# A hybrid decoder layer on one core: the sixteen buffers of the normalized x spaced 4160 bytes apart instead of 4096, with one buffer less in two other rings

## The chip, the core and the metric

The kernel runs on one core of a Trainium2 chip. The metric is device time in microseconds (us) of one execution, as a median over runs. On-chip memory has 128 partitions; every buffer below is counted in bytes of one partition.

## The reference, cut to what matters

One decoder layer over a sequence of 2048 tokens of width 1024, all in float32:

```python
u = rmsnorm(h, norm_mix_w);  proj = u @ w_in
# four heads of a gated linear recurrence (hq, hf, hi, hg), chunk by chunk
o_hg = rmsnorm(hgrn2_chunkwise(q, k, v, log_f)) * silu(hg)
# eight heads of sliding-window attention (window 128) with a sink logit
o_att = sliding_window_attention_with_sinks(aq, ak, av, sinks)
h = h + concat(o_hg, o_att) @ w_out
v = rmsnorm(h, norm_ffn_w)
gate = causal_depthwise_conv(v @ w_gate, conv_w, conv_b)
h = h + (silu(gate) * (v @ w_up)) @ w_down
return rmsnorm(h, final_norm_w)
```

## The kernel before, in words

The sequence is done in two halves of 1024 tokens (`HALF`), channels on the partitions. Each half is a mixing stage (the four recurrence heads of `hgrn`, interleaved with the four attention steps of `attend`), the output projection `out_proj`, the gate and up projections `gate_up`, and the down projection `down`, which also loads the x of the next half.

**Precision by splitting.** A float32 operand is kept as two tiles, a rounded high part and the remainder (`split`, `prep`, `split_into`). Each product is three matmuls: high by high (L790, L1000), remainder of the moving operand (L791, L1001), remainder of the weights (L792, L1002). In `unit` (L190 to L209) all three stand in L208, with the two 512-column halves of x behind each other. In the profile's `out<-in` the moving operand stands first and the weights second: `hq<-XH,whi` streams XH through the array with weights whi.

**The x buffers.** `new_x` (L211) takes one buffer from the ring `xh` and one from the ring `xl` of the pool `xp`, eight each (`KT`), 4096 bytes a buffer. They hold XH and XL, the scaled x of the mixing stage. The same sixteen buffers are taken again later under other names: by `Operands.get` (L636) for the operands T2, T3, B22 and T4 of the feed-forward (in the profile T and B), and by `prep_piece` in `down` (L953) for the reloaded activations (xhd, xld). B11, T1 and B21 live elsewhere, in the rings `xh2` and `xl2` of the feed-forward's pool. `project_v` (L601) is the one place where XH and XL are the weights and a prepared weight streams past them.

**Where buffers lie.** Pools follow one another in memory: const, x, w, h, small, then the pool of the stage (`mix0`, `ffn0`, `mix1`, `ffn1`). x, w and h hold nothing but buffers of 4096 bytes: inv, xh and xl, then raw, hi and lo, then the eight slots `m`. So in the program before, every one of these starts at the same place modulo 4096: the first xh buffer at byte 28992, which is 320 modulo 4096, and the xl buffers, raw, whi, wlo and the slots at 320 as well. The small pool shifts what comes behind it: xh2 and xl2 start at 1088 modulo 4096. The ring `ga` of the feed-forward has two buffers of `2 + HALF` floats (4104 bytes, laid out at a distance of 4128): they begin at bytes 220224 and 224352. The first is a multiple of 64, the second lies 32 behind a multiple of 64. `ga` serves as a gate tile and, in `down`, as a home of weights for every third piece (L958, `k % 3 == 2`; `gad` in the profile: high part in the first buffer, remainder in the second).

**The level keys.** Within a recurrence head, `hgrn` goes through seven levels m = 1, 2, 4 ... 64 (L503). For m < 32 and the first three heads of a half, `pairs` (L475) copies every second run of K into a tile KK of 2048 bytes on ScalarE (L479) and runs four matmuls on it (L482, two passes each in the trace). Then Q is updated (L522, VectorE, after those matmuls), K (L523, after the copy) and the gates F (L529); `place_pairs` copies half of the result (`moved`, L489), sends it through a DMA issued from ScalarE (L492, and L494 for m = 1), and writes both halves into ST (L498, L501). KK has `KB` = 2 buffers, so the copy of one level can be made while the matmuls of the level before still have theirs to read. That makes 5 copies a head, 30 in all, and 24 times that one level hands over to the next.

**The small ring.** `ut` has `UT` = 7 buffers of 2048 bytes: the copies out of PSUM in `pair_unit` (s1, u2, s5, u3, L797), the squares of the statistics (sq, fsq, L238), t1 (L695), v7 (L677), and S1, S2 and S4 of the first weight pair (L744).

The order of instructions on each engine's queue is made by the tile framework when the program is built: it simulates the program with its own costs and gives out buffers as they come free (`schedule_with_timeline_sim=True`), so the number of buffers of a ring takes part in the order.

Of the kernel before, what the change touches and what calls it, by code (L numbers as in the profile page):

```python
# [9 lines left out]
F32R = mybir.dt.float32r  # L10
# [7 lines left out]
P = 128  # L18
D = 1024
KT = D // P  # L20
S = 2048
HALF = 1024
# [15 lines left out]
BEHIND = {1: {0: 1}, 2: {0: "pu", 2: "po", 5: "pot"}}  # L38
LEVELS = [1, 2, 4, 8, 16, 32, 64]
NEG = -1.0e30  # L40
UT = 7
RAW = 3
VB = 2
KB = 2
WARM = 12
LV = 4

# [2 lines left out]
def hymba_layer(ctx: ExitStack, tc: tile.TileContext, a: dict, out: bass.AP):  # L50
    nc = tc.nc

    def pool(name, bufs=1, space=None, stack=ctx, **kw):
        if space is not None:
            kw["space"] = space
        return stack.enter_context(tc.tile_pool(name=name, bufs=bufs, **kw))

    cp = pool("const")
    xp = pool("x")
# [14 lines left out]
    def halves():  # L74
        return [(b, slice(b * 512, (b + 1) * 512)) for b in range(NB)]
# [133 lines left out]
        return o  # L209

    def new_x():  # L211
        return (xp.tile([P, HALF], F32R, tag="xh", name="XH", bufs=KT),
                xp.tile([P, HALF], F32R, tag="xl", name="XL", bufs=KT))

    def split(src, w=None, eng=None, dst=None):

        h, l = dst or new_x()
        if w is None:
            nc.scalar.copy(h, src)
            (eng or nc.vector).tensor_tensor(l, src, h.bitcast(F32), op=ALU.subtract)  # L220
        else:
            nc.scalar.activation(h, src, AF.Identity, scale=w)
            nc.vector.scalar_tensor_tensor(l, src, w, h.bitcast(F32), op0=ALU.mult, op1=ALU.subtract)
        return h, l
# [43 lines left out]
    def inv_tile():  # L268
        return xp.tile([P, HALF], F32, tag="inv", name="invb", bufs=1)
# [5 lines left out]
    def load(hf, X, stage, W=None):  # L275

        st = Stats(inv_tile())
        xt = []

        def part(kt, c):  # L280
            nc.sync.dma_start(xt[kt][:, c], a["xT"][kt, :, hf * HALF + c.start:hf * HALF + c.stop])
            split(xt[kt][:, c], nmw[:, kt:kt + 1], dst=[t[:, c] for t in X[kt]])

        for kt in range(KT):
            xt.append(stage())
            X.append(new_x())
            if W is not None and kt == 0:

                parts = [lambda c=c: part(0, c) for _, c in halves()]
                W.append(prep(a["w_att"][ATT_J], parts=(slice(0, P), slice(P, D)), between=parts))  # L290
                for p_ in parts:
                    p_()
            else:
                part(kt, slice(0, HALF))
            if W is not None and kt == 1:
                W.append(prep(a["w_att"][ATT_J + 1]))

            if W is None:
                st.add(xt[kt])
            elif kt >= 3:  # L300
                st.add(xt[kt - 3])
            yield st
        for kt in range(KT - 3, KT) if W is not None else ():
            st.add(xt[kt])
# [38 lines left out]
    def attend(hf, j, X, invb, KS, V, mix, p):  # L343
# [58 lines left out]
        for g, sc in enumerate(scs):  # L402
            pm = []
            for kv in range(2):
                pm.append([p.tile([P, 4, P], F32, tag="pp", name=n, bufs=4) for n in ("po", "pp")])
                pt = ps("at", "ppt")
                for i in range(4):
                    nc.tensor.transpose(pt[:, i * P:(i + 1) * P], sc[:, kv, i], ident)
                ptv = pt.rearrange("p (i q) -> p i q", i=4)
                for dst, mk in zip(pm[kv], (C.ownT, C.prevT)):  # L410
                    nc.vector.tensor_tensor(dst, ptv, mk.unsqueeze(1).to_broadcast([P, 4, P]), op=ALU.mult)
            oT = ps("at", "poT")
            for i in range(4):
                n = g * 4 + i
                noprev = hf == 0 and n == 0
                for prev in range(1 if noprev else 2):
                    for kv in range(2):
                        r = rows(kv)
                        nc.tensor.matmul(oT[r, i * P:(i + 1) * P], V[:, n + 1 - prev, r], pm[kv][prev][:, i],
                                         start=prev == 0, stop=noprev or prev == 1)  # L420
            gs = slice(g * 512, (g + 1) * 512)
            if j < ATT_J - 1:
                nc.scalar.copy(qT[:, gs], oT)
                mix[4 + j] = qT
            else:
                if g == 0:
                    mix[4 + j] = new_x()
                h, l = mix[4 + j]
                nc.scalar.copy(h[:, gs], oT)
                nc.vector.tensor_tensor(l[:, gs], oT, h[:, gs].bitcast(F32), op=ALU.subtract)  # L430
            yield

    def hgrn(hf, h, X, invb, vs, WG, mix, p, fu=None):
# [41 lines left out]
        def pairs():  # L475


            KK = p.tile([P, HALF // 2], F32, tag="KK", name="KK", bufs=KB)
            nc.scalar.copy(KK.rearrange("p (r b c m) -> p r c b m", r=TT // 2, c=2, m=m),  # L479
# [138 lines left out]
    def split_into(h, l, src, eng=None):  # L618
        return (nc.scalar.copy(h, src),  # L619
                (eng or nc.vector).tensor_tensor(l, src, h.bitcast(F32), op=ALU.subtract))  # L620
# [25 lines left out]
    def out_proj(hf, M, p):  # L646
# [4 lines left out]
        st = Stats(acc)  # L651
        sts = [Stats(acc[:, bs], lambda: p.tile([P, 512], F32, tag="ut", name="sq", bufs=UT)) for _, bs in halves()]
        ops = Operands(p)
# [5 lines left out]
        for d in range(KT):  # L659
# [5 lines left out]
            if d == KT - 2:  # L665
# [3 lines left out]
                                  lambda n: p.tile([P, D], F32R, tag="ga", name=n, bufs=2),  # L669
                                  lambda n: p.tile([P, 512], F32, tag="ut", name=n, bufs=UT))  # L670
            if d >= len(W):
# [4 lines left out]
            u = v[d - 4] if d >= 4 else None  # L676
            w = [t[:, bs] if d < KT - 1 else p.tile([P, 512], F32, tag="ut", name="v7", bufs=UT) for _, bs in halves()]  # L677
            sums = []
# [14 lines left out]
            if d < 4:  # L693
                split_into(*ops.get("B11", d), t[:, lo])
                t1 = p.tile([P, 512], F32, tag="ut", name="t1", bufs=UT)  # L695
                nc.vector.tensor_tensor(t1, t[:, hi], t[:, lo], op=ALU.subtract)
# [77 lines left out]
    def pair_unit(W, ops, p, evac, then={}, behind_first=None):  # L774
# [20 lines left out]
        def out(o, name):  # L795
            t = p.tile([P, 512], F32, tag="ut", name=name, bufs=UT)
            copied[:] = [nc.scalar.copy(t, o)]  # L797
            return t
# [119 lines left out]
    def down(hf, kept, acts, p):  # L918
# [89 lines left out]
        for k, (name, _, _, j) in enumerate(todo):  # L1008
            if k + 2 < len(todo):
                ready[k + 2] = prep_piece(k + 2)  # L1010
            if j == 0:
# [6 lines left out]
                if name == "P3":  # L1018
                    acc = inv_tile() if final else wp.tile([P, HALF], F32, tag="raw", name="sums", bufs=RAW)
                    s1, s2 = [Stats(acc[:, bs], lambda: p.tile([P, 512], F32, tag="ut", name="fsq", bufs=UT))  # L1020
                              for bs in (lo, hi)]
# [186 lines left out]
```

## Time and profile before

| what | us |
|---|---|
| median of 2 runs (2203.91 to 2204.89) | 2204.4 |
| the profiled execution's own time | 2203.92 |
| its span, first to last instruction | 2202.2 |
| TensorE (PE) busy | 2177.6 |
| VectorE (DVE) busy | 1644.0 |
| ScalarE (ACT) busy | 1050.4 |

The profile comes from one execution. PE is TensorE's matmul stream, PEld its weight loads, which run beside it; DVE is VectorE, ACT ScalarE, SP the engine that issues most DMAs. A row of the groups gives line, engine, operation, names and shape, then count, busy us, mean ns, and the idle time before it with what ended that. Matmuls are pipelined: a matmul of 512 columns is shown as 389 ns long while the next one starts 0.227 us behind it, so the pace is read from starts and the 389 only compares like with like. The mean granted TensorE clock of this execution is 0.997.

### The profile page before, as it was taken

Reading aid. Unit: us, or ns where it says so; the run is one execution under the profiler, and the core shown is the slowest. Engines: PE = TensorE matmul, PEld = TensorE weight load, DVE = VectorE, ACT = ScalarE, POOL = GpSimd, SP = SyncE. Lnnn points to the kernel's source line nnn. Section 1 sums busy time; section 2 is a strip of 40 time slices with the busy share of each in tenths; the row PEclk is TensorE's granted clock in tenths of the full one; section 3 lists DMA queues with packets and bytes.
Section 4 is the critical chain, followed back from the end, with each engine's and each line's share of the span. In section 5 each row is a group of like instructions: output and inputs, shape, how many; then the busy total and the mean of one; then the engine's idle time right before and its main releaser. Section 6 shows DMA issues by size and latency. Waiting matters only on the chain.

```text
span 2202.2 us, 29514 instructions
## 1 busy us (share of the span) xinstructions
PE 2177.6 (99%) x11406; PEld 1829.1 (83%) x11406; DVE 1644.0 (75%) x2490; ACT 1050.4 (48%) x1845; POOL 6.5 (0%) x27
## 2 busy tenths in 40 slices
PE   9999999999999999999999999999999999999998
PEld 7988988888888888888889889888888888888887
DVE  6568568688887888775856666577888888887766
ACT  6446554464444445335625455535634444453353
POOL 1000000000000000000000000000000000000000
PEclk9999999999999999999999999999999999999999
DMA  4111112323333334964631111204132323359643
GB/s 154 50 30 50 37 43 68 124 68 113 96 112 101 96 120 157 374 224 162 202 125 46 39 36 50 68 29 140 52 134 86 128 83 120 96 192 391 223 136 129
DMA packets 94214, 257.91 MB, mean 117 GB/s; under 512 B 11578, under 2 KB 17402, under 8 KB 94074
## 3 DMA queue, kind: packets, MB, share of 16 engines
q1 hardware_dynamic: 88128, 251.70, 33.9%
q10 hardware_dynamic: 5946, 4.34, 0.7%
q8 instruction: 89, 1.46, 0.3%
q14 instruction: 51, 0.42, 0.1%
HBM read 195.10 MB, written 57.15 MB: 115 GB/s over the span
## 4 chain that ended last, share of the span: by engine, by line
PE 94%; DVE 3%; ACT 1%; DMA 1%; issue 0%; ACTq 0%; DVEq 0%
PE X L790 7%; PE X L791 7%; PE X L792 7%; PE pop L208 7%; PE hq L208 4%; PE q L208 4%; PE f L208 4%; PE g L208 4%; PE Y L792 4%; PE Y L791 4%; PE Y L790 4%; PE pdx L1000 3%; PE pdx L1001 3%; PE pdx L1002 3%; PE pdy L1001 3%; PE pdy L1000 3%
## 5 line engine op out<-in xcount | busy, mean ns | idle before, releaser
L619 ACT CAST whi<-raw 128x1024 fp32r<-128x1024 f32 x88 | 92.7, 1053 | 109.3 <-PE X L791 67.6
L790 PE MATMUL X<-T,whi 128*128 128x512 f32 x352 | 136.9, 389 | 0.0
L791 PE MATMUL X<-T,whi 128*128 128x512 f32 x352 | 136.9, 389 | 0.0
L792 PE MATMUL X<-T,wlo 128*128 128x512 f32 x352 | 136.9, 389 | 0.0
L884 DVE SCALAR_TENSOR_TENSOR y<-ga,cw,y 128x1024 f32<-128x1024 f32 x88 | 112.4, 1279 | 26.0 <-ACT y L882 25.9
L797 ACT COPY u<-X 128x512 f32<-128x512 f32 x88 | 51.6, 586 | 133.9 <-PE X L792 133.7
L620 DVE TENSOR_TENSOR wlo<-raw,whi 128x1024 fp32r<-128x1024 f32 x88 | 107.2, 1218 | 0.0
L184 ACT CAST whi<-raw 128x1024 fp32r<-128x1024 f32 (+2 forms) x61 | 62.7, 1034 | 80.1 <-PE q L208 31.9
L620 DVE TENSOR_TENSOR xld<-raw,xhd 128x1024 fp32r<-128x1024 f32 x72 | 80.8, 1132 | 18.5 <-ACT xhd L619 18.2
L619 ACT CAST xhd<-raw 128x1024 fp32r<-128x1024 f32 x72 | 69.6, 977 | 41.7 <-DMA raw<-act1T 13.5
L208 PE MATMUL pop<-XL,whi 128*128 128x512 f32 x256 | 85.3, 393 | 2.1 <-DVE XL L220 2.1
L208 PE MATMUL pop<-XH,wlo 128*128 128x512 f32 x256 | 84.7, 391 | 0.8 <-DVE wlo L185 0.8
L208 PE MATMUL pop<-XH,whi 128*128 128x512 f32 x256 | 83.9, 395 | 0.2
L185 DVE TENSOR_TENSOR wlo<-raw,whi 128x1024 fp32r<-128x1024 f32 (+2 forms) x61 | 73.1, 1204 | 8.1 <-ACT whi L184 8.1
L790 PEld LDWEIGHTS X<-T,whi 128*128 128x128 f32 x352 | 66.1, 188 | 13.7
L791 PEld LDWEIGHTS X<-T,whi 128*128 128x128 f32 x352 | 66.1, 188 | 13.7
L792 PEld LDWEIGHTS X<-T,wlo 128*128 128x128 f32 x352 | 66.0, 188 | 13.7
L1000 PE MATMUL pdx<-xhd,hid 128*128 128x512 f32 x192 | 74.5, 391 | 1.0 <-ACT hid L619 1.0
L1001 PE MATMUL pdx<-xld,hid 128*128 128x512 f32 x192 | 74.8, 390 | 0.0
L1002 PE MATMUL pdx<-xhd,lod 128*128 128x512 f32 x192 | 73.7, 389 | 0.0
L611 PE MATMUL pvv<-whi,XH 128*128 128x256 f32 x256 | 73.5, 288 | 0.0
L612 PE MATMUL pvv<-whi,XL 128*128 128x256 f32 x256 | 72.7, 285 | 0.0
(363 smaller groups left out, 6555.8 us busy)
## 6 DMA issues: line engine op xcount, KB each, us to landing
wr<-in_w_down SPq DMA_DIRECT2D x90, 512.0 KB, 5.0
raw<-in_w_gate SPq DMA_DIRECT2D x44, 512.0 KB, 3.6
raw<-in_w_up SPq DMA_DIRECT2D x44, 512.0 KB, 3.6
raw<-act0T SPq DMA_DIRECT2D x20, 512.0 KB, 5.7
raw<-act1T SPq DMA_DIRECT2D x20, 512.0 KB, 10.2
act0B<-y SPq DMA_DIRECT2D x33, 256.0 KB, 2.6
act1B<-y SPq DMA_DIRECT2D x33, 256.0 KB, 2.4
raw<-in_w_out SPq DMA_DIRECT2D x16, 512.0 KB, 4.6
```

Source lines behind the costliest of these rows:

```text
L185: nc.vector.tensor_tensor(lo[:, c], raw[:, c], hi[:, c].bitcast(F32), op=ALU.subtract)
L208: nc.tensor.matmul(o[b], w, x[:, bs], start=f, stop=l)
L611: nc.tensor.matmul(o[:, 0:256], xh[:, t], hi[:, c], start=kt == 0, stop=False)
L619: return (nc.scalar.copy(h, src), (eng or nc.vector).tensor_tensor(l, src, h.bitcast(F32), op=ALU.subtract))
L620: (eng or nc.vector).tensor_tensor(l, src, h.bitcast(F32), op=ALU.subtract))
L790: nc.tensor.matmul(o, wh[:, ws], xh, start=i == 0 and not more, stop=False, skip_group_check=more)
L791: nc.tensor.matmul(o, wh[:, ws], xl, start=False, stop=False, skip_group_check=more)
L792: r = nc.tensor.matmul(o, wl[:, ws], xh, start=False, stop=i == 3, skip_group_check=more)
L884: nc.vector.scalar_tensor_tensor(y, g[:, w:w + HALF], C.cw[:, ft, w:w + 1], y, op0=ALU.mult, op1=ALU.add)
L1000: nc.tensor.matmul(o, wh[:, i, c], ah[:, i, cols], start=f, stop=False, skip_group_check=more)
L1001: nc.tensor.matmul(o, wh[:, i, c], al[:, i, cols], start=False, stop=False, skip_group_check=more)
L1002: nc.tensor.matmul(o, wl[:, i, c], ah[:, i, cols], start=False, stop=l, skip_group_check=more)
```

## The change

`new_x` takes tiles of 1040 floats and hands out their first 1024. Ring buffers are as long as the longest tile of their ring, so each xh and xl buffer becomes 4160 bytes, whoever uses it: the k-th of the sixteen moves on by 64 k bytes, all stay multiples of 64, and all that lies behind them moves by 1024 bytes. To stay within the memory, `UT` goes from 7 to 6 and `KB` from 2 to 1 (2048 bytes each). `ga` and what follows it in the feed-forward's pool so lie 1024 bytes earlier than before, and keep their places modulo 64. No instruction is added or taken away by the text of the change.

```diff
-UT = 7
+UT = 6
 RAW = 3
 VB = 2
-KB = 2
+KB = 1
...
     def new_x():
-        return (xp.tile([P, HALF], F32R, tag="xh", name="XH", bufs=KT),
-                xp.tile([P, HALF], F32R, tag="xl", name="XL", bufs=KT))
+
+        return tuple(xp.tile([P, HALF + 16], F32R, tag=t, name=t.upper(), bufs=KT)[:, 0:HALF] for t in ("xh", "xl"))
```

## The prediction

> **What bounds the kernel now.** First the page's span and busy times, then the chain that ended last: which engine carries the time, and how much of it is waiting.
>
> ```profile
> span 2202.2 us, 29514 instructions
> PE 2177.6 (99%) x11406; PEld 1829.1 (83%) x11406; DVE 1644.0 (75%) x2490; ACT 1050.4 (48%) x1845; POOL 6.5 (0%) x27
> PE 94%; DVE 3%; ACT 1%; DMA 1%; issue 0%; ACTq 0%; DVEq 0%
> ```
>
> TensorE is the bound. It is busy for 2177.6 of 2202.2 us, so 24.6 us is all that better hiding could bring in the whole program. A change that adds no work on PE can move the time in two ways: it changes the pace of a matmul, or it makes PE wait. The waits of PE, longest first, show where it waits today:
>
> ```profile
> PE pinv L263 <- DVE invb L253: 2.9, 1, 2.9
> PE kv L208 <- ACT XH L222: 2.3, 3, 1.3
> ...
> PE plev L515 <- DVE K L523: 2.1, 2, 1.4
> ```
>
> No wait is for a buffer of KK or of ut: the longest is 2.9 us, once. The pace is read from starts in the timeline, first in the mixing stage (x moving, weights in whi and wlo), then in the down projection with weights in `ga`:
>
> ```profile
> 59.91 0.62 PE L208 MATMUL q<-XL,whi 128*128 128x512 f32 x2
> 60.36 0.62 PE L208 MATMUL q<-XH,wlo 128*128 128x512 f32 x2
> 60.82 0.61 PE L208 MATMUL q<-XH,whi 128*128 128x512 f32 x2
> 61.27 0.62 PE L208 MATMUL q<-XL,whi 128*128 128x512 f32 x2
> ```
>
> ```profile
> 925.37 0.40 PE L1000 MATMUL pdy<-xhd,gad 128*128 128x512 f32 x1
> 925.60 0.40 PE L1001 MATMUL pdy<-xld,gad 128*128 128x512 f32 x1
> 925.84 0.39 PE L1002 MATMUL pdy<-xhd,gad 128*128 128x512 f32 x1
> 926.07 0.40 PE L1000 MATMUL pdy<-xhd,gad 128*128 128x512 f32 x1
> ```
>
> From 59.91 to 61.27 six matmuls of 512 columns start: 1.36/6 = 0.227 us each. From 925.37 to 926.07 three: 0.70/3 = 0.233 us, and the middle one has 0.84 - 0.60 = 0.24 us. So the place of a buffer can cost time on PE. That is the question which the change asks of the x buffers.
>
> **The change, part by part.**
>
> *The sixteen x buffers.* The groups that stream an x buffer, one of each three lines, with their counts:
>
> ```profile
> L790 PE MATMUL X<-T,whi 128*128 128x512 f32 x352 | 136.9, 389 | 0.0
> L790 PE MATMUL X<-T,Sh 128*128 128x512 f32 x176 | 68.8, 391 | 1.5 <-ACT s L797 1.5
> L790 PE MATMUL Y<-B,S 128*128 128x512 f32 x176 | 68.5, 389 | 0.0
> L208 PE MATMUL pop<-XH,whi 128*128 128x512 f32 x256 | 83.9, 395 | 0.2
> L208 PE MATMUL hq<-XL,whi 128*128 128x512 f32 x128 | 43.7, 401 | 0.0
> L1000 PE MATMUL pdx<-xhd,hid 128*128 128x512 f32 x192 | 74.5, 391 | 1.0 <-ACT hid L619 1.0
> L1000 PE MATMUL pdy<-xhd,hid 128*128 128x512 f32 x160 | 62.3, 389 | 0.0
> L1001 PE MATMUL pdx<-xld,gad 128*128 128x512 f32 x72 | 28.8, 400 | 0.0
> ```
>
> f, q and g have 128 a row, as hq. Per line that is 352 + 176 + 176 + 256 + 4 x 128 + 192 + 160 + 72 = 1896, and three lines make 5688, some 5700 matmuls (smaller groups left out). Each nanosecond on every one of them is 5.7 us.
>
> What does it take to change their pace? Three comparisons in the trace of before:
>
> ```profile
> L790 PE MATMUL Y<-T,Sh 128*128 128x512 f32 x176 | 68.5, 389 | 0.0
> L790 PE MATMUL X<-B,whi 128*128 128x512 f32 x176 | 68.5, 389 | 0.0
> L1000 PE MATMUL pdx<-xhd,xh2d 128*128 128x256 f32 x88 | 24.6, 284 | 0.0
> L611 PE MATMUL pvv<-whi,XH 128*128 128x256 f32 x256 | 73.5, 288 | 0.0
> ```
>
> Y<-T,Sh and this X<-B,whi stream T1 and B11 out of the rings xh2 and xl2, which start at 1088 modulo 4096; the weights lie at 320 plus a multiple of 512. X<-T,whi streams from the x ring, at 320 like its weights. All three show 389 ns: equal residues cost nothing that a difference of 768 would save. The other way round, with weights at 1088 and x moving at 320 (pdx<-xhd,xh2d), 256 columns show 284 ns, against 288 where both lie at 320 (pvv). Only the `gad` rows stand out, and there the buffer that is off is the second of `ga`, 32 bytes behind a multiple of 64: the matmul during which it is loaded (L1001, the next one needs the remainder of the weights) shows 400 ns, 11 more than 389. The first `ga` buffer has yet another residue (3136), but it is a multiple of 64, and where it alone is loaded (L1002, the next weight is again the high part) the timeline above shows the pace of all others: 0.23 us from 925.84 to 926.07. I read this as a matter of the place within 64 bytes, not of the residue modulo 4096. The change moves x by multiples of 64 and leaves all others at their place modulo 64. Value taken: 0.
>
> Bounds: the upper one is the worst `gad` matmul on all of them, 11 ns each, which is 5700 x 0.011 = 63 us. The lower one is the excess that the mixing stage's own groups show over 389, worst in hq<-XL,whi with 401: 12 ns on the 4 x 3 x 128 = 1536 matmuls of f, hq, q and g is 18 us, of which the waits listed above are a part. I take 0 because the rows of equal and unequal residues at multiples of 64 agree to the nanosecond.
>
> [...]
>
> DVE and ACT write the x buffers (L222, L223, L619, L620) and read raw and whi at 320. They are at 75% and 48%, so a change in their pace would first have to eat their slack: cost 0.
>
> *KB from 2 to 1.* With two buffers the copy for a level is made ahead. ScalarE, PE and VectorE around the first hand-over of the first head:
>
> ```profile
> 74.82 0.67 ACT L479 COPY KK<-K 128x512 f32<-128x512 f32 x1
> 76.83 0.37 ACT L489 COPY moved<-plev 128x256 f32<-128x256 f32 x1
> 77.23 1.38 ACTq L492 DMA_DIRECT2D odd<-moved  x1
> 78.65 0.58 ACTq L494 DMA_DIRECT2D odd<-moved  x1
> ```
>
> ```profile
> 75.72 1.07 PE L482 MATMUL plev<-Q,KK 128*128 128x128 f32 x8
> ...
> 79.86 0.84 PE L482 MATMUL plev<-Q,KK 128*128 128x128 f32 x6
> ```
>
> ```profile
> 78.73 0.69 DVE L523 TENSOR_TENSOR K<-K,f 128x512 f32<-128x512 f32 x1
> ```
>
> The matmuls of level 1 end at 75.72 + 1.07 = 76.79, those of level 2 start at 79.86: 3.07 us, which PE fills with project_v. With one buffer the copy for level 2 (74.82 now) has to come behind 76.79. If it goes first on ScalarE it is done at 76.83 + 0.67 = 77.5, with 2.3 us to spare. If it is queued behind `moved` and the two DMA issues it starts at 78.65 + 0.58 = 79.23 and is done at about 79.9, that is 0.04 us too late for PE; the K update of level 2 (78.73), which overwrites what the copy reads, then comes 1.2 us later on VectorE, and behind it only the next level's work. Levels from 2 on have one DMA issue, not two, and so 0.58 us more slack. Six heads have a first hand-over. I take 1 us in all: 6 x (0.04 late and twice the 0.04 that the signal from PE's end at 76.79 to ScalarE's start at 76.83 takes) is 0.7, rounded up. Ends: 0 with the copy first, and 24 hand-overs x 0.67 (the whole copy exposed each time) = 16 us. The other 6 copies (first level of a head) find the buffer free since long.
>
> *UT from 7 to 6.* The ring is fullest where the gate projection starts:
>
> ```profile
> 465.87 1.15 ACT L238 ACTIVATE sq<-h 128x512 f32<-128x512 f32 x2
> 467.26 0.59 ACT L797 COPY s<-Y 128x512 f32<-128x512 f32 x1 [0.24 <-PE Y L792]
> 470.06 0.59 ACT L797 COPY u<-X 128x512 f32<-128x512 f32 x1
> ```
>
> ```profile
> 467.03 1.28 DVE L241 TENSOR_TENSOR invb<-invb,sq 128x512 f32<-128x512 f32 x2
> ```
>
> When s5 is copied out at 467.26, the tiles in use are S4, one v7, s1, the two sq and s5 itself: six. The two sq are free at 467.03 + 1.28 = 468.3, before u2 at 470.06. So six buffers are just enough; one late would wait for the first sq, about 0.4 us, twice (two halves). In the steady loop a unit of 84 matmuls (7 products of 12, 84 x 0.227 = 19 us) has four such tiles. Value 0, ends 0 and 0.8 us.
>
> *The order of the queues.* Fewer buffers can make the framework order the queues otherwise. That has no row; its ends are today's PE idle time of 24.6 us below, and as much above; nearest to it are the single waits of 1 to 3 us above, so I take 0.
>
> **Sum.** 2203.92 (the profiled execution, 0.5 us under the median of 2204.4) + 0 + 1 + 0 + 0 = 2204.9, or 2205 us.
>
> **Rivals.**
>
> *The x buffers come to stand as badly as the second `ga` buffer* (slower). Place: the 5700 matmuls above. Price: between 0.233 (mean of a `gad` triple) and 0.238: 5700 x 0.006 = 34 us, 2239, up to 63 us, 2268. Beyond 44/5700 = 7.7 ns a matmul it is slower by over 2%. For it: the `gad` rows. Against: the rings at 1088.
>
> *The level keys show.* 24 hand-overs of 0.67 us, 16 us, 2221; for it the 0.04 us above, against it that PE has project_v, q and g to put in between.
>
> *The mixing stage's excess goes* (faster). If x and the weights at one residue are what makes hq 401 and not 389, a third to all of 18 us: 2186 to 2199. For it: only mixing rows show the excess. Against: the feed-forward's rows have the same equal residues and 389.
>
> *Nothing changes but the order*: 2198 to 2212, the change not doing what its words say.
>
> **Chances.** No change beyond the order, 2198 to 2212: 0.70. Level keys or order above that, to 2228: 0.13. As `ga`: 0.09, of that 0.05 over 2% (above 7.7 ns). Faster by the mixing stage's excess: 0.08; since its bound is 18 us, 0.01 over 2% is left for what no row shows. The range of 8 in 10 is 2197 to 2224. Faster by over 2% (about what a measurement of this kernel can tell from no change) 0.01, within 2% 0.94, slower 0.05.
>
> **What would show it.** X<-T,whi at 389 ns and 0.227 us from start to start: the spacing does nothing; 395 or more: the first rival. The hq and f rows going from 401 to 389: the third. Waits of `plev L482` for `ACT KK L479` in PE's list: the level keys. Waits of `Y` or `X` for `s L797` above 1.5 us: the small ring. The prediction is wrong if PE busy moves by more than 10 us, or if its idle time leaves 20 to 40 us.

## The result, and the profile after

The changed kernel takes 2227.3 us (median of 2 runs, 2226.6 to 2228.0) against 2204.4: a ratio of 1.0106 [1.009, 1.0122], 22.9 us more. The forecast was 2205, with a range that ended at 2224.

First the page of the changed kernel: its span, the busy times and the chain that ended last by engine.

```profile
span 2226.2 us, 29552 instructions
PE 2203.3 (99%) x11406; PEld 1827.7 (82%) x11406; DVE 1644.9 (74%) x2490; ACT 1048.7 (47%) x1845; POOL 6.2 (0%) x27
PE 95%; DVE 3%; DMA 1%; ACT 1%; issue 0%; ACTq 0%; DVEq 0%
```

The span grew by 24.0 us and PE's busy time by 25.7, with the same 11406 matmuls. PE's idle time went from 24.6 to 2226.2 - 2203.3 = 22.9 us. So the time did not go into waiting: the matmuls themselves became slower. The mean granted TensorE clock is 0.997 in both kernels. PE's longest waits in the changed kernel say the same. None is for a KK; the one for the copy s (L797), the prediction's sign for the small ring, was 1.5 us before and is 1.4 now:

```profile
PE pinv L263 <- DVE invb L253: 2.9, 1, 2.9
PE kv L208 <- ACT XH L222: 1.8, 2, 1.4
...
PE X L790 <- ACT s L797: 1.4, 2, 0.7
...
PE plev L515 <- DVE K L523: 1.3, 2, 0.6
```

Which matmuls? The groups of the changed kernel by line and shape (count, busy us, mean ns):

```profile
L790 PE MATMUL X<-T,whi 128*128 128x512 f32 x352 | 138.5, 394 | 0.0
L208 PE MATMUL pop<-XH,whi 128*128 128x512 f32 x256 | 85.5, 399 | 0.2
L611 PE MATMUL pvv<-whi,XH 128*128 128x256 f32 x256 | 72.3, 283 | 0.0
L790 PE MATMUL X<-T,Sh 128*128 128x512 f32 x176 | 69.5, 395 | 1.4 <-ACT s L797 1.4
L790 PE MATMUL X<-B,whi 128*128 128x512 f32 x176 | 68.9, 391 | 0.0
L790 PE MATMUL Y<-T,Sh 128*128 128x512 f32 x176 | 68.8, 391 | 0.0
L1000 PE MATMUL pdx<-xhd,hid 128*128 128x512 f32 x192 | 75.1, 394 | 1.0 <-ACT hid L619 1.0
L208 PE MATMUL hq<-XL,whi 128*128 128x512 f32 x128 | 44.1, 403 | 0.0
L1001 PE MATMUL pdx<-xld,gad 128*128 128x512 f32 x72 | 28.4, 395 | 0.0
```

The groups of 512 columns that stream from the sixteen buffers are 2 to 5 ns longer (X<-T,whi was 389, pop 395, X<-T,Sh 391, hq 401). Two exceptions teach as much: the L1001 row of `gad`, where the second `ga` buffer had been the odd one, fell from 400 to 395, and pvv, where the x buffers are the weights, from 288 to 283. X<-B,whi and Y<-T,Sh stream from rings that were not spread out, and still show 391 instead of 389.

The pace shows it in the timeline of the mixing stage, where each product goes through eight buffers in turn; here three neighbours, whose x buffers stand 64, 0 and 192 bytes above their weights, modulo 256 (by the addresses of the built program):

```profile
59.19 0.61 PE L208 MATMUL hq<-XH,whi 128*128 128x512 f32 x2
...
60.56 0.63 PE L208 MATMUL q<-XH,whi 128*128 128x512 f32 x2
...
61.95 0.63 PE L208 MATMUL q<-XH,whi 128*128 128x512 f32 x2
...
63.35 0.63 PE L208 MATMUL q<-XH,whi 128*128 128x512 f32 x2
...
```

Six matmuls a buffer: 1.37/6 = 0.228, 1.39/6 = 0.232 and 1.40/6 = 0.233 us, where before all ran at 0.227. The buffer with equal places is slow too, which is taken up below.

Summed from start to start over the whole trace, the 7930 matmuls of 512 columns take 1836.5 us before and 1861.1 after (+24.6), those of 256 columns 161.3 and 158.4 (-2.8), those of 128 columns 151.8 and 154.5 (+2.8, differences taken before rounding). Together that is +24.6 us; those of 64 columns give 0.6 back, and the spans are 24.0 apart.

### The profile page after: what moved, and what is told of

Same layout as the page of the kernel before. It is cut to its first block, busy times and chain, and to the rows that moved or that the text cites. A ratio compares the mean times of both kernels' runs of the same rounds, so it can differ in the third digit from the quotient of the medians.

```text
span 2226.2 us, 29552 instructions
## 1 busy us (share of the span) xinstructions
PE 2203.3 (99%) x11406; PEld 1827.7 (82%) x11406; DVE 1644.9 (74%) x2490; ACT 1048.7 (47%) x1845; POOL 6.2 (0%) x27
## 4 chain that ended last, share of the span: by engine, by line
PE 95%; DVE 3%; DMA 1%; ACT 1%; issue 0%; ACTq 0%; DVEq 0%
PE X L790 7%; PE X L791 7%; PE X L792 7%; PE pop L208 7%; PE hq L208 4%; PE q L208 4%; PE f L208 4%; PE pdx L1000 4%; PE Y L792 4%; PE pdx L1002 4%; PE pdx L1001 4%; PE Y L790 4%; PE Y L791 4%; PE g L208 4%; PE pdy L1001 3%; PE pdy L1000 3%
## 5 line engine op out<-in xcount | busy, mean ns | idle before, releaser
L797 ACT COPY u<-X 128x512 f32<-128x512 f32 x88 | 51.4, 584 | 145.5 <-PE X L792 144.9
L1000 PE MATMUL pdx<-xhd,hid 128*128 128x512 f32 x192 | 75.1, 394 | 1.0 <-ACT hid L619 1.0
L1001 PE MATMUL pdx<-xld,hid 128*128 128x512 f32 x192 | 75.2, 392 | 0.0
L1002 PE MATMUL pdx<-xhd,lod 128*128 128x512 f32 x192 | 74.4, 392 | 0.0
```

Source lines behind the costliest of these rows:

```text
L1000: nc.tensor.matmul(o, wh[:, i, c], ah[:, i, cols], start=f, stop=False, skip_group_check=more)
L1001: nc.tensor.matmul(o, wh[:, i, c], al[:, i, cols], start=False, stop=False, skip_group_check=more)
L1002: nc.tensor.matmul(o, wl[:, i, c], ah[:, i, cols], start=False, stop=l, skip_group_check=more)
```

## The experiments

**The theory.** All x and weight buffers of the kernel before start at 64 modulo 256 (320 and 1088 both do, and the first `ga` buffer at 3136 too). Spread 64 bytes apart, three of every four x buffers stand elsewhere than their weights modulo 256, and matmuls of 512 columns then run slower. By "distance" I mean the place of the moving operand minus that of its weights, modulo 256; the second `ga` buffer, at 96, puts an x at 64 at a distance of 224. Rivals: the smaller rings and the order that follows from them; the longer stride by itself; a place that is bad whatever the weights have; other engines' traffic to the same memory.

**1. The rings alone.**

```diff
-UT = 7
+UT = 6
...
-KB = 2
+KB = 1
```

> The two smaller rings alone (UT 6, KB 1), x buffers back at a distance of 4096; the order of all queues is then that of the changed kernel. Theory A (the place of the x buffers costs pace on PE): 2203 to 2207 us, X<-T,whi at 389 ns. Theory B (the smaller rings and the order they bring cost it): 2225 to 2229 us, with PE's waits or the mixing stage longer.

Measured: 2205.4 us against 2204.05 of before, 1.0007 [0.9998, 1.0016]; X<-T,whi 389 ns. Its instructions stand in the order of the changed kernel, so ring and order together cost 1.4 us, not surely more than nothing. Against this run the sums of the changed kernel differ by +25.3 us (512 columns), -2.1 (256) and -0.2 (128): 23.0, with spans 22.9 apart. The 3 us in 128 columns belong to the rings, all the rest to the spacing.

**2. The change with a step of 256 instead of 64.**

```diff
-        return tuple(xp.tile([P, HALF + 16], F32R, tag=t, name=t.upper(), bufs=KT)[:, 0:HALF] for t in ("xh", "xl"))
+        return tuple(xp.tile([P, HALF + n], F32R, tag=t, name=t.upper(), bufs=KT)[:, 0:HALF] for t, n in (("xh", 64), ("xl", 0)))
```

> As the changed kernel, same rings and same order, but the eight xh buffers are 4352 bytes apart and the eight xl ones 4096: the residues modulo 4096 differ, those modulo 256 are all equal. Theory A1 (what counts is the distance of x and weights modulo 256): within 2 us of the run with the smaller rings alone. Theory A2 (any difference modulo 4096 costs): 12 to 24 us more than it, as half or all of the buffers are off.

Measured: 2206.3 us, 1.0010 [1.0000, 1.0019]. From the groups of this run:

```profile
L790 PE MATMUL X<-T,whi 128*128 128x512 f32 x352 | 136.9, 389 | 0.0
```

The xh buffers are spread over eight places modulo 4096 and X<-T,whi is back at 389. A spread in multiples of 256, here up to 7 x 256, costs nothing that shows (0.9 us over run 1); neither do longer buffers as such.

**3 to 6. The kernel before, with x moved against its weights, or both together.** A pad ahead of the x pool moves all that follows; a second pad ahead of the weights' pool brings these back to 64 modulo 256. The numbers shown are those of the 128-byte run; 64 and 192, and 192 and 64, make the two others, and 192 ahead of x alone moves x and weights together.

```diff
+    for q, n in ((xp, 128), (wp, 128),):
+        nc.gpsimd.memset(q.tile([P, n // 4], F32, name="pad"), 0.0)
```

> The kernel before, with a pad of 128 bytes ahead of the x pool and one of 128 behind it: all sixteen x buffers 128 bytes off the weights modulo 256, nothing else moved modulo 256, rings and order of before. Theory A1: in the changed kernel a quarter of the buffers stands so, and if the 23 us come evenly from three quarters of them, 5 ns on some 5700 matmuls: 2228 to 2238 us, every group that streams x at 394 ns or more. Theory B: 2204 us.

> The kernel before with a pad of 192 bytes ahead of everything in x and behind: x, weights, xh2, xl2 and ga all move together, to residue 0 modulo 256, where the changed kernel's worst buffers stand. Theory A1 (distance between x and weights counts): 2203 to 2206 us, 389 ns. Rival A3 (the place itself counts, for each operand alone): X<-T,whi at 394 ns or more, 2230 to 2245 us.

> As the run with x 128 bytes off the weights, but 64 bytes. Theory A1 with a cost that does not depend on the distance: 2234 to 2237 us again. A1 with a cost that grows with the distance round the 256 bytes (64 and 192 alike, 128 the worst): 2215 to 2228 us.

> As the run with x 128 bytes off the weights, but 192 bytes, which is 64 in the other direction. Cost that does not depend on the distance: 2234 to 2237 us. Cost by distance round the 256 bytes: the same time as at 64. Cost that depends on which of the two lies ahead: another time than at 64, by 5 us or more.

Measured, and per x matmul the excess over before divided by the 5700 of the prediction:

| distance of x from its weights | us (before beside it) | ratio | ns a matmul |
|---|---|---|---|
| 64 | 2217.6 (2204.1) | 1.0061 [1.0046, 1.0077] | 2.4 |
| 128 | 2235.6 (2204.05) | 1.0139 [1.0124, 1.0154] | 5.5 |
| 192 | 2234.9 (2204.1) | 1.0141 [1.0127, 1.0155] | 5.4 |
| both moved by 192: 0 | 2204.25 (2204.05) | 1.0001 [0.9991, 1.0010] | 0.0 |

The groups of the 128-byte run:

```profile
L790 PE MATMUL X<-T,whi 128*128 128x512 f32 x352 | 138.8, 394 | 0.0
L1001 PE MATMUL pdy<-xld,hid 128*128 128x512 f32 x160 | 63.2, 395 | 0.0
L790 PE MATMUL Y<-T,Sh 128*128 128x512 f32 x176 | 68.7, 390 | 0.0
```

and of the run in which both moved by 192:

```profile
L790 PE MATMUL X<-T,whi 128*128 128x512 f32 x352 | 136.9, 389 | 0.0
```

It is the distance between the moving operand and the weights that counts, not where either lies. The column of ns charges all of the excess to the x matmuls; run 11 shows that some of it falls on others. Rings and the order on PE, DVE, ACT and SP are those of before in all four.

**7 and 8. The `ga` ring of the kernel before**, with the second buffer 4352 bytes behind the first (so equal modulo 256), and 4160 (64 off).

```diff
-            ga = [p.tile([P, 2 + HALF], F32, tag="ga", name="ga", bufs=2) for _ in range(2)]
+            ga = [p.tile([P, 1088], F32, tag="ga", name="ga", bufs=2)[:, 0:2 + HALF] for _ in range(2)]
```

> The kernel before, only the two ga buffers 4352 bytes apart instead of 4128, so that the second stands at the same place modulo 256 as all other weights. Theory A1: pdx<-xld,gad falls from 400 to 389 ns, its triples from 0.233 to 0.227 us a matmul: some 470 matmuls x 6.5 ns = 3 us less, 2201 us. Rival (it was another thing than the place that made these rows slow, such as the length of the pieces): 400 ns and 2204 us as before.

> The kernel before, the two ga buffers 4160 bytes apart: the second is a multiple of 64 now, but 64 bytes off the others modulo 256. The reading of the prediction (the place within 64 bytes is what costs): 389 ns and 2201 us, as with 4352. Theory A1 (the distance modulo 256): pdx<-xld,gad stays above 389, at 393 to 400, 2203 to 2204 us.

Measured: 2200.1 us with 4352, 0.9983 [0.9974, 0.9992], faster than both kernels; 2203.1 with 4160, 0.9995 [0.9986, 1.0004]. The `gad` rows with 4352 (before: 394 in L1000, 400 in L1001 and 389 in L1002):

```profile
L1001 PE MATMUL pdx<-xld,gad 128*128 128x512 f32 x72 | 28.0, 389 | 0.0
L1002 PE MATMUL pdx<-xhd,gad 128*128 128x512 f32 x72 | 28.0, 389 | 0.0
L1000 PE MATMUL pdx<-xhd,gad 128*128 128x512 f32 x72 | 28.0, 389 | 0.0
```

and with 4160 (1040 in place of 1088 in the edit; L1000 is at 389):

```profile
L1002 PE MATMUL pdx<-xhd,gad 128*128 128x512 f32 x72 | 28.6, 398 | 0.0
L1001 PE MATMUL pdx<-xld,gad 128*128 128x512 f32 x72 | 28.2, 392 | 0.0
```

With equal places the excess of `gad` is gone. With 64 off, which is a distance of 192, it is still there, although this buffer is now a multiple of 64; the time itself cannot be told from before. "The place within 64 bytes", the reading in the prediction, is refuted here too.

**9. TensorE alone.** Ahead of the whole program, stretches of 48 matmuls on private operands; the offset of the moving tile, in floats of 4 bytes, differs (the rings UT, KB and LV are made smaller to hold the two tiles).

```diff
...
+    def probe(name, count, off, cols=512, ws=(0, 0)):
+        o = ps("mm", name)
+        for i in range(count):
+            w = ws[i % 2] + (i // 2 % 2 * 128 if max(ws) < 128 else 0)
+            nc.tensor.matmul(o[:, 0:cols], pw[:, w:w + P], pm[:, off:off + cols], start=i == 0, stop=i + 1 == count)
+
+    probe("lead", 200, 0)
+    for name, off in (("pa", 0), ("pb", 8), ("pc", 16), ("pd", 32), ("pe", 48), ("pf", 64)):
+        probe(name, 48, off)
+    probe("pg", 48, 0, ws=(0, 16))
+    for name, off in (("ph", 0), ("pi", 32)):
+        probe(name, 48, off, 256)
...
```

> The kernel before with fewer tiles in three rings (UT 5, KB 1, LV 3), which makes room for a private moving tile and private weights; ahead of everything else 200 + 9 x 48 added matmuls run while the other engines have nothing to do. Distances of the moving operand from the weights: pa 0, pb 32, pc 64, pd 128, pe 192, pf 256 bytes with 512 columns, ph 0 and pi 128 with 256 columns; pg has its weights alternately at 0 and 64. Theory A (TensorE's own two reads, the moving operand and the next weights, get in each other's way when their places differ modulo 256): pa and pf 0.227 us from start to start, pc 0.229, pd and pe 0.232 to 0.233, pb 0.233 or more; ph and pi alike. Rival B (traffic of other engines or of the DMAs to the same memory is needed): 0.227 in all 512-column stretches.

The whole run, one execution, takes 2335 us, some 131 more than before. Its timeline (start, length, engine, line, operation, count):

```profile
51.96 11.04 PE L114 MATMUL pa<-pm,pw 128*128 128x512 f32 x48
62.84 11.37 PE L114 MATMUL pb<-pm,pw 128*128 128x512 f32 x48
74.04 11.16 PE L114 MATMUL pc<-pm,pw 128*128 128x512 f32 x48
85.04 11.32 PE L114 MATMUL pd<-pm,pw 128*128 128x512 f32 x48
96.19 11.36 PE L114 MATMUL pe<-pm,pw 128*128 128x512 f32 x48
107.39 11.09 PE L114 MATMUL pf<-pm,pw 128*128 128x512 f32 x48
118.31 11.20 PE L114 MATMUL pg<-pm,pw 128*128 128x512 f32 x48
129.35 5.92 PE L114 MATMUL ph<-pm,pw 128*128 128x256 f32 x48
135.10 5.86 PE L114 MATMUL pi<-pm,pw 128*128 128x256 f32 x48
140.80 0.61 PE L227 MATMUL kv<-XH,whi 128*128 128x512 f32 x2
```

and what the engines did in most of that stretch (busy us of PE, PEld, DVE, ACT and POOL, then granted clock, DMA share and GB/s):

```profile
64.00:107.00 43.00, 43.00 (x187) 34.84 (x186) 0.00 (x0) 0.00 (x0) 0.00 (x0) 1.00 0.00 1
```

From start to start, divided by 48: 226.7 ns at distance 0 (pa), 233.3 at 32, 229.2 at 64, 232.3 at 128, 233.3 at 192, 227.5 at 256. No other engine ran, the DMA share is 0.00 and the clock 1.00. So nobody else's traffic is needed. In pg the weights change with every matmul between their place and 64 bytes above it, so the distance alternates between 0 and 192: 230.0 is just the mean of 226.7 and 233.3. Whether other mixtures cost more than their mean is the question of run 11. The excess, 2.5, 5.6 and 6.6 ns at 64, 128 and 192, is near the 2.4, 5.5 and 5.4 of the whole kernel, though those hold other things too: there, matmuls of 256 columns took 3.0, 0.8 and 2.2 us less than before.

**10. x at a distance of 32.** The edit of run 3 with 32 and 224.

> The kernel before with 32 bytes of padding ahead of the x buffers and 224 ahead of the weights: only the x buffers stand elsewhere modulo 256, at 96 where their weights stand at 64. Theory A (any difference modulo 256 costs, and 32 costs as in the second ga buffer): making that buffer equal saved 4.3 us on 252 matmuls, 17 ns each by the time, and 10.7 ns each by the durations of its rows (400, 394 and 389 over both buffers), so 5700 of them would give 2265 to 2300 us, X<-T,whi at 395 or more. Rival C (32 costs no more than 64 does, and the second ga buffer was dear for being a weight buffer): 2218 us. Rival D (only multiples of 64 count): 2204 us.

Measured: 2239.3 us against 2204.5, 1.0158 [1.0141, 1.0175], 34.8/5700 = 6.1 ns a matmul, near the probe's 6.6. The distance matters as expected, but the size, 2265 to 2300, was missed. I had charged the excess of the `gad` rows to half of their matmuls. Spread over all of them it is (394 + 400 + 389)/3 - 389 = 5.3 ns, and by the prediction's own starts 0.233 - 0.227 = 0.006 us, which fits the 6.1; run 11 shows why all of them count.

**11. A mixture of distances.** The probe's frame, 96 matmuls a stretch.

```diff
...
+    four = (0, 16, 32, 48)
+    probe("lead", 200, (0,))
+    probe("qa", 96, (0,))
+    probe("qb", 96, four)
+    probe("qc", 96, four, 12)
+    probe("qd", 96, (0,), 1, (0, 0, 8))
+    probe("qe", 96, (0,), 1, (8, 8, 8))
+    probe("qf", 96, (0,), 1, (0, 0, 16))
+    probe("qg", 96, (0,), 1, (16, 16, 16))
...
```

> The frame of the run before, with other stretches, each 96 added matmuls of 512 columns: qa all at distance 0; qb with the moving operand 0, 64, 128, 192 bytes on, changing with every matmul, qc the same changing every 12 (as in the unit products); qd with the weights of one matmul in three 32 bytes on (as with the second ga buffer), qe with all of them 32 on; qf one in three 64 on, qg all 64 on. Theory M (a change of the distance costs by itself, as the 18 ns of a ga triple with one set of weights off against the 18 ns of three x matmuls off suggest): qd costs as much over qa as qe does, 6 ns a matmul, and qb lies above the mean of the four distances (230.6 ns), at 232 or more. Theory N (each matmul pays for its own distance, and only that): qd a third of qe, 229 ns where qe is 233; qf a third of qg; qb and qc both at 230.6.

One execution, 2400.85 us. Its timeline, in the same columns:

```profile
51.94 21.70 PE L115 MATMUL qa<-pm,pw 128*128 128x512 f32 x95
73.48 22.41 PE L115 MATMUL qb<-pm,pw 128*128 128x512 f32 x96
95.73 22.34 PE L115 MATMUL qc<-pm,pw 128*128 128x512 f32 x96
117.91 22.54 PE L115 MATMUL qd<-pm,pw 128*128 128x512 f32 x96
140.29 22.56 PE L115 MATMUL qe<-pm,pw 128*128 128x512 f32 x96
162.69 22.34 PE L115 MATMUL qf<-pm,pw 128*128 128x512 f32 x96
184.87 22.56 PE L115 MATMUL qg<-pm,pw 128*128 128x512 f32 x96
207.26 0.62 PE L231 MATMUL kv<-XH,whi 128*128 128x512 f32 x2
```

From start to start: qa 226.7, qd 233.1, qe 233.3, qf 231.0, and qg, up to the start of kv, 233.2. Weights 32 bytes on mean a distance of 224, weights 64 on one of 192. So qg agrees with pe of run 9 (233.3), where the moving operand was the one moved: again only the distance counts. One set of weights in three at 224 costs all but as much as three in three (6.4 of 6.6 ns); at 192 it is 4.3 of 6.5 where a third would be 2.2. A matmul thus does not pay for its own distance alone: a neighbour at another distance makes the equal ones slow as well. The mixtures of four, qb 231.8 and qc 231.0, lie above the mean of the single distances, (226.7 + 229.2 + 232.3 + 233.3)/4 = 230.4. That qb would reach 232 was not quite met. pg, which lay at its mean, shows that not every mixture costs more.

Single starts in the trace show how long a neighbour counts. In qc the distance changes every twelve matmuls. Where it returns from 192 to 0, the first five matmuls are 226, 236, 228, 233 and 231 ns from the next start, and only the seven behind them 226 or 227. The kernel shows the same in rows whose own distance no edit changed: some 1580 matmuls that stream B11, B21 and T1 (X<-B,whi, Z<-B,whi, Y<-T,Sh and their remainders), all but eight at distance 0 throughout. From start to start they take 226.8 ns before and in runs 1, 2 and 4, but 229.2 in the changed kernel, and 230.2, 228.2, 228.5 and 229.5 in the runs with x at 64, 128, 192 and 32.

## Why the prediction was wrong

*The x buffers, value 0: this step failed.* It rested on "the rows of equal and unequal residues at multiples of 64 agree to the nanosecond". The unequal pair was 1088 and 320, whose difference is 768 = 3 x 256. Distances that are multiples of 256 cost nothing that lasts (0.9 us in run 2, 227.5 against 226.7 ns in run 9), so the comparison had set equal against equal, and the trace of before held no difference of 64, 128 or 192 between an x buffer and its weights. The one odd distance in it, the second `ga` buffer, is odd modulo 256 as well as modulo 64, and I chose the second reading; runs 3, 5, 6 and 8, all at multiples of 64 (5.5, 2.4 and 5.4 ns a matmul more, and 398 against 389 ns in L1002), show that it was the wrong one. The flaw was in the bounds of the evidence, not in the arithmetic: "unequal" was seen at one number only, and the change brings others. The prediction also put the 400 of L1001 down to the loading of the odd weights; in run 8 it is L1002, which uses them, that stands out (398 ns, and 392 in L1001), so the loading alone does not tell which of the three pays.

What the term measures: with the rings and the order alike, the spacing costs 2227.3 - 2205.4 = 21.9 us (run 1). Put together from parts: an even quarter of the x matmuls at each distance, priced by the whole-kernel runs 3 to 6, gives (0 + 13.6 + 31.6 + 30.9)/4 = 19.0 us. The mixture adds, by qc, 231.0 - 230.4 = 0.6 ns on 5700 matmuls, an estimate of 3.4 us. With the 1.4 of the rings that is 23.8, against 22.9 measured; the closeness is in part luck, as the 19.0 already holds what the neighbours of x lost in those runs.

For those neighbours the prediction had no term at all. The 1580 matmuls of run 11's last paragraph take 3.8 us more in the changed kernel and no more in runs 1, 2 and 4, so it is the place of x that slows them. The slow buffer at distance 0 in the timeline fits too: in the mixing stage x changes its buffer every six matmuls, and qc needs up to five to recover. Why a neighbour counts for so long stays open.

*The first rival, "as badly as the second `ga` buffer", was the right cause*, with 0.09 of the chances. Its price, 6 to 11 ns on all 5700 (34 to 63 us), is met at its lower end where all of x is at one bad distance: 31 to 35 us in runs 3, 6 and 10. In the change a quarter of x stays at 0 and a quarter at the cheap 64. Its sign was "395 or more" on X<-T,whi; it came to 394.

*The cause, as far as it shows.* Run 9 goes further than the `gad` rows (400 against 389 ns): with every other engine idle (DVE, ACT and POOL 0.00 us busy, DMA share 0.00 from 64 to 107 us) the pace goes from 226.7 to 233.3 ns by the distance between the two operands alone. That the reads of moving operand and next weights get in each other's way is the nearest reading, and not shown: every matmul has a weight load of its own (11406 of each in both kernels, 187 and 186 in that stretch of run 9), and no run shows what happens inside the memory.

*KB, 1 us, and UT, 0: right in size.* Together they measured 1.4, with an interval that includes 0. The worry about KB, that the copy would queue behind `moved` and two DMA issues, came half true. ScalarE in the changed kernel:

```profile
78.13 0.37 ACT L489 COPY moved<-plev 128x256 f32<-128x256 f32 x1 [0.30 <-PE plev L482]
78.53 0.66 ACT L479 COPY KK<-K 128x512 f32<-128x512 f32 x1
78.54 1.40 ACTq L492 DMA_DIRECT2D odd<-moved  x1
```

The copy comes behind `moved`, but it runs beside the issue (78.53 and 78.54), so it is done at 79.19 and PE has no wait for it.

*The third rival* (the excess of the mixing rows over 389 goes) fell: hq is at 403, not 389. *The signs*: the text said that it would be wrong if PE busy moved by more than 10 us. It moved by 25.7, while the idle time stayed within its 20 to 40; this told at once that pace, not waiting, was the matter.

## What to carry to other kernels

Before changing the address of an operand that TensorE streams, work out its distance from its weights modulo 256, and keep it at zero (here 2200.1 us with the second `ga` buffer made equal, 2218 to 2239 with x off). This was measured with float32 operands, weights of 128 x 128 and 512 columns; other shapes and types need a measurement of their own. When a row is to show that a difference doesn't matter, ask which differences it really contains, and under which moduli two "unequal" numbers are equal. A single odd buffer in three can cost nearly as much as three (6.4 of 6.6 ns), so look at small rings whose tiles are a few bytes longer than a round number.

## What was not expected of the hardware

The price doesn't grow with the distance: 32 bytes cost 6.6 ns on a 512-column matmul, 64 cost 2.5, 128 cost 5.6, 192 and 224 again 6.6. At 256 the mean is 227.5 against 226.7, and the difference lies in the first ten matmuls of the stretch, behind one at 192; the others are at 226 or 227. With 256 columns it is, in one stretch, the other way round: ph, at distance 0, takes (135.10 - 129.35)/48 = 119.8 ns, and pi, at 128, (140.80 - 135.10)/48 = 118.8; the changed kernel's matmuls of 256 columns took 2.8 us less in all, and pvv went from 288 to 283 ns.
